# An eighth pair of buffers for the weighted expert products of a decoder block, and two small tiles fewer

## The chip, the cores and the metric

The kernel runs on one core of one Trainium2 chip. What is measured is the time of one execution on the device, in microseconds (us).

## What is computed

One block of a hybrid decoder on 1024 tokens of width 1024: two attention mixers, an attention to 256 memory tokens, and a channel mixer (PEER) with 16384 experts. Only the channel mixer matters here. Each token chooses 128 experts (8 heads of 16) and gets their weighted sum:

```python
a = jnp.einsum('cd,ced->ce', hc, u[ic])                  # first products: token times chosen rows of u
a = jax.nn.gelu(a, approximate=False) * gc               # weighted
return jnp.einsum('ce,ced->cd', a, v[ic])                # second products: weighted sum of chosen rows of v
```

All is in float32, with every product of large matrices made of three matmuls of a high and a low part (`mm3`, lines 135 to 137).

## The kernel before, in words

The channel mixer goes two ways at once. For tokens 0 to 511 (four blocks of 128) the chosen rows of u and v are **gathered**: GpSimd (POOL) issues an indirect DMA of 128 rows (512 KB), and VectorE (DVE) multiplies them with the tokens (line 1038, the u half) or adds them, weighted, to a sum (line 1057, the v half). There are 4 x 128 gathers of each kind, through 7 buffers `rows`. `gathered_u` leaves 128 first products per token in a tile `aa`, `gathered_v` makes weights `wexp` of it with a Gelu on ScalarE (ACT, line 1045) and a product with the gates (line 1046). The gathers are spread over the program beside other work.

For tokens 512 to 1023 the products are **dense** (function `dense`): all 16384 experts, in 128 steps of 128 experts, with the weight 0 for experts that a token did not choose. The weights lie in DRAM (`Wd`). A step has two halves.

- First products (`first`): the u rows of the step are loaded (`uraw`, 512 KB), split into a high part on ACT and a low part on DVE (`uT0`, `uT1`), and TensorE (PE) runs 24 matmuls into a PSUM tile `acc`. ACT applies Gelu (line 1253), DVE multiplies with the weights `wl` from `Wd` (line 1254; one load, 512 KB, serves two steps; there are two buffers `wl`), and the product is split again: high part `c0` on ACT (line 112), low part `c1` on DVE (line 113).
- Second products (`second`): the v rows are loaded (`vraw`) and split into `v0` (ACT) and `v1` (DVE), four buffers each, and PE runs 24 matmuls on `c0`, `c1`, `v0`, `v1`, into 8 PSUM outputs: four stay there (`kept`), four go through two buffers `out`, from which DVE adds them to a sum in SBUF (`accu`, line 1288).

Four steps make a **group**; there are 32. In a group's second half each of the 8 outputs takes 12 matmuls, so every one of its four `c` pairs is read until the last output. `group` of the next group is written ahead of `second` of this one, so that PE has the next first products or the next second products to go on with.

The first products of 48 steps, that is of 12 groups, were already made in an earlier stage and stored in DRAM (`ga`, after the Gelu). These **early groups** only load them (`c`, line 1250, one buffer of 256 KB) and multiply with `wl`. They are mixed among the others: the list `order` puts an early group at the places 2, 5, 7, 10, 13, 15, 18, 21, 23, 26, 29 and 31 (from 0).

So at 12 places PE finds no first products between two second halves. Call the groups around such a place P, X and E: E is early, X is the group ahead of it in the order, P the one ahead of X. PE goes from the second half of P straight to that of X; this is called a **crossing** below. X's steps are 0 to 3, and so are E's.

What stands on which engine in which order is set by a scheduler from the program's dependencies and its own costs; each engine then runs its queue in that order, and SyncE (SP) issues the loads in its own. A buffer that is not yet free makes the instruction that writes it wait, and what stands behind it on that queue. With `bufs=7`, four pairs `c0`, `c1` hold P's products and three X's; the pair of X's step 3 has to wait for the end of P's second half.

```python
w = w2[:, :, e % 2]                                                          # 1247: half of a tile wl
nc.vector.tensor_tensor(w, c.rearrange(...), w, op=OP.mult)                  # 1254
ch = [sp.tile([P, DT], F32R, name=f"c{j}", bufs=7) for j in range(2)]        # 1255
self.split(w, *[x.rearrange(...) for x in ch])                               # 1256
```

## Time and profile before

| what | value |
|---|---|
| median of 3 runs | 3581.61 us (3581.43 to 3586.86) |
| the profiled execution: its own time | 3578.94 us |
| the profiled execution: span of its instructions | 3577.2 us |
| busy in the span | PE 3049.6 us, DVE 2853.5 us, ACT 1405.0 us, POOL 1391.8 us |
| mean granted clock of PE | 0.921 of full speed |
| the dense loop | 2219 to 3545 us |

Times are microseconds from the span's start. An engine's idle time is put down to what ended it (the releaser). Matmuls overlap, so a sum of their durations is more than the time that they take in a row.

### The profile page before, as it was taken

What the parts mean: (1) busy time and instruction counts of PE and PEld (TensorE: products, weight loads), DVE (VectorE), ACT (ScalarE), POOL (GpSimd) and SP (SyncE); (2) the same over time, 40 slices, a digit from 0 to 9 for tenths busy, and PEclk for the clock granted to TensorE, in tenths of its full rate; (3) what the DMA queues carried; (4) which work ended last, traced back from release to release, by engine and by line L of the source; (5) the groups of instructions that cost most, each with busy time, mean ns of one, the idle gap of its engine ahead of it and who ended that gap; (6) DMA issues with size and microseconds to landing.
All of it is one profiled execution on the core that took longest, in us unless ns stands there. A gap on an engine that the chain in (4) does not pass through costs nothing. (4 is left out here: it accounts for less than half of the span.)

```text
span 3577.2 us, 42240 instructions
## 1 busy us (share of the span) xinstructions
PE 3049.6 (85%) x13234; PEld 2306.6 (64%) x13234; DVE 2853.5 (80%) x6623; ACT 1405.0 (39%) x2537; POOL 1391.8 (39%) x1122
## 2 busy tenths in 40 slices
PE   8999888798697997776998975888989898888995
PEld 7778756453355856465766764766777777676874
DVE  6656544698799889978998997887888888788987
ACT  5756344256575622132555564222222232222212
POOL 0010000002255265651125654465645546555554
PEclk9999989899897998888999988999999999899998
DMA  4584534436898398986569999999999999899987
GB/s 135 159 199 121 184 110 157 130 102 214 242 303 283 111 347 315 329 311 232 199 225 349 375 396 383 323 345 320 353 321 322 312 332 342 299 326 348 365 305 262
DMA packets 394209, 964.64 MB, mean 270 GB/s; under 512 B 36712, under 2 KB 146048, under 8 KB 392576
## 3 DMA queue, kind: packets, MB, share of 16 engines
q0 software_dynamic: 155264, 560.01, 44.7%
q1 hardware_dynamic: 238720, 401.94, 32.8%
q8 instruction: 104, 1.70, 0.2%
q14 instruction: 121, 0.99, 0.1%
HBM read 871.64 MB, written 90.18 MB: 269 GB/s over the span
## 5 line engine op out<-in xcount | busy, mean ns | idle before, releaser
L1035 POOL DMA_INDIRECT rows<-in_peer_u_dram,ii x512 | 681.2, 1331 | 925.6 <-DVE rows L1038 316.4
L1051 POOL DMA_INDIRECT rows<-in_peer_v_dram,ii x512 | 647.4, 1265 | 505.2 <-DVE h3s L1057 346.3
L1057 DVE SCALAR_TENSOR_TENSOR h3s<-rows,wexp,h3s 128x1024 f32<-128x1024 f32 x508 | 651.0, 1282 | 27.5 <-DMA rows<-in_peer_v_dram,ii 17.8
L1038 DVE SCALAR_TENSOR_TENSOR rows<-rows,h3s 128x1024 f32<-128x1024 f32 x512 | 610.3, 1217 | 61.4 <-DMA rows<-in_peer_u_dram,ii 59.8
L135 PE MATMUL acc<-fT,uT 128*128 128x512 f32 x1024 | 421.1, 411 | 65.5 <-DVE wl L1254 45.3
L137 PE MATMUL acc<-fT,uT 128*128 128x512 f32 x1024 | 412.2, 403 | 4.1 <-DVE uT L113 4.0
L136 PE MATMUL acc<-fT,uT 128*128 128x512 f32 x1024 | 413.7, 404 | 0.0
L112 ACT ACTIVATE c<-wl 128x512 fp32r<-128x512 f32 x128 | 79.4, 629 | 813.8 <-PE out L136 463.0
L135 PEld LDWEIGHTS acc<-fT,uT 128*128 128x128 f32 x1024 | 198.5, 194 | 112.6 <-issue 29.5
L149 POOL TENSOR_TENSOR rstd<-msq,mhalf 128x1 f32<-128x1 f32 (+1 forms) x42 | 34.1, 812 | 593.1 <-DVE msq L147 582.5
L136 PE MATMUL kept<-v,c 128*128 128x512 f32 x512 | 209.5, 410 | 61.3 <-DVE v L113 61.3
L135 PE MATMUL out<-v,c 128*128 128x512 f32 x512 | 210.7, 412 | 56.1 <-DVE accu L1288 56.1
L112 ACT ACTIVATE uT<-uraw 128x1024 fp32r<-128x1024 f32 x128 | 135.6, 1059 | 254.5 <-PE acc L136 194.5
L137 PEld LDWEIGHTS acc<-fT,uT 128*128 128x128 f32 x1024 | 197.4, 193 | 58.0 <-issue 11.2
L136 PEld LDWEIGHTS acc<-fT,uT 128*128 128x128 f32 x1024 | 198.4, 194 | 40.2 <-issue 0.8
L113 DVE TENSOR_TENSOR w<-wraw,w 128x512 fp32r<-128x512 f32 (+1 forms) x176 | 116.7, 679 | 116.8 <-ACT w L112 110.0
L137 PE MATMUL kept<-v,c 128*128 128x512 f32 x512 | 206.3, 403 | 0.0
L136 PE MATMUL out<-v,c 128*128 128x512 f32 x512 | 205.7, 402 | 0.0
L137 PE MATMUL out<-v,c 128*128 128x512 f32 x512 | 205.3, 401 | 0.0
L135 PE MATMUL kept<-v,c 128*128 128x512 f32 x512 | 203.5, 406 | 0.0
L568 ACT ACTIVATE junk<-W,xb 128x384 bf16<-128x384 f32 (+5 forms) x186 | 163.7, 880 | 77.0 <-DVE xb L566 65.5
L133 PE MATMUL acc<-wraw,hT 128*128 128x512 f32 (+1 forms) x384 | 170.4, 598 | 11.3 <-ACT tok L355 7.6
(361 smaller groups left out, 6717.8 us busy)
## 6 DMA issues: line engine op xcount, KB each, us to landing
uraw<-in_peer_ut_dram SPq DMA_DIRECT2D x128, 512.0 KB
vraw<-in_peer_v_dram SPq DMA_DIRECT2D x128, 512.0 KB
Wd<-wbuf SPq DMA_DIRECT2D x64, 512.0 KB
wl<-Wd SPq DMA_DIRECT2D x64, 512.0 KB
wraw<-in_w_in_dram SPq DMA_DIRECT2D x40, 512.0 KB
fraw<-in_w_in_dram SPq DMA_DIRECT2D x32, 512.0 KB
wraw<-in_w_out_dram SPq DMA_DIRECT2D x24, 512.0 KB
ga<-gelu SPq DMA_DIRECT2D x48, 256.0 KB
```

What stands on the lines that cost most here:

```text
L112: self.nc.scalar.activation(hi, src, AF.Copy)
L113: self.last_dve = self.nc.vector.tensor_tensor(lo, src, hi.bitcast(F32), op=OP.subtract).ins
L133: self.last_pe = nc.tensor.matmul(out, l[0], r[0], start=start, stop=stop).ins
L135: nc.tensor.matmul(out, l[0], r[0], start=start, stop=False)
L136: nc.tensor.matmul(out, l[0], r[1], start=False, stop=False)
L137: self.last_pe = nc.tensor.matmul(out, l[1], r[0], start=False, stop=stop).ins
L149: nc.gpsimd.tensor_tensor(r, v, self.mhalf[:, :n], op=OP.pow)
L568: nc.scalar.activation(junk[:, :(b + 1) * P], self.W[b], AF.Sign, bias=xb[:, j:j + 1].bitcast(F32), accum_out=s[:, j:j + 1])
L1035: nc.gpsimd.indirect_dma_start(out=u, out_offset=None, in_=a["peer_u"][0], in_offset=bass.IndirectOffsetOnAxis(ap=ii[:, j:j + 1], axis=0))
L1038: nc.vector.scalar_tensor_tensor(u, u, 1.0, h3, op0=OP.mult, op1=OP.mult, accum_out=aa[:, j:j + 1])
L1051: nc.gpsimd.indirect_dma_start(out=v, out_offset=None, in_=a["peer_v"][0], in_offset=bass.IndirectOffsetOnAxis(ap=r["ii"][:, j:j + 1], axi ...
L1057: nc.vector.scalar_tensor_tensor(o, v, w[:, j:j + 1], o, op0=OP.mult, op1=OP.add)
```

## The change

The pairs `c0`, `c1` get an eighth buffer (4 KB more per partition). To make room, `aa` has two buffers in place of three, and `gathered_v` makes its weights in place, in `aa`, so that `wexp` goes.

```diff
-        aa = r["aa"] = ep.tile([P, P], F32, name="aa", bufs=3)
+        aa = r["aa"] = ep.tile([P, P], F32, name="aa", bufs=2)
...
-        w = ep.tile([P, P], F32, name="wexp", bufs=1)
-        nc.scalar.activation(w, r["aa"], AF.Gelu)
+        w = r["aa"]
+        nc.scalar.activation(w, w, AF.Gelu)
         nc.vector.tensor_tensor(w, w, r["gg"], op=OP.mult)
...
-                    ch = [sp.tile([P, DT], F32R, name=f"c{j}", bufs=7) for j in range(2)]
+                    ch = [sp.tile([P, DT], F32R, name=f"c{j}", bufs=8) for j in range(2)]
```

No instruction is added or taken away, but the scheduler writes the queues in another order, at the crossings. Three places of the crossing at 2589 to 2640 us of the trace follow (its E is the fourth early group; P's `wl` is not in them, X's second tile is `wl_21477` before and `wl_21475` now, E's two tiles are `wl_21730` and `wl_21746` before and `wl_21727` and `wl_21743` now).

DVE at the crossing, before. `c1_21565` is X's step 3, `c1_21736`, `c1_21743` and `c1_21752` are E's steps 0 to 2, the `v1` are X's:

```order
L113 TENSOR_TENSOR c1_21565<-wl_21477,c0_21564 128x512
L1288 TENSOR_TENSOR accu_18901<-accu_18901,out_21713 128x512
L113 TENSOR_TENSOR c1_21736<-wl_21730,c0_21735 128x512
L113 TENSOR_TENSOR c1_21743<-wl_21730,c0_21742 128x512
L113 TENSOR_TENSOR v1_21763<-vraw_21764,v0_21762 128x1024
L113 TENSOR_TENSOR v1_21769<-vraw_21770,v0_21768 128x1024
L1254 TENSOR_TENSOR wl_21746<-c_21748,wl_21746 128x8x64
L113 TENSOR_TENSOR v1_21775<-vraw_21776,v0_21774 128x1024
L113 TENSOR_TENSOR c1_21752<-wl_21746,c0_21751 128x512
L113 TENSOR_TENSOR v1_21781<-vraw_21782,v0_21780 128x1024
```

X's step 3 is split at the crossing, and E's product of step 2, with the tile `wl_21746` that this split sets free, stands in the midst of X's four `v1`.

DVE in P's second half, ahead of the crossing, now. `c1_21563` is X's step 3, the products (line 1254) are E's steps 1 and 2:

```order
L1254 TENSOR_TENSOR wl_21727<-c_21736,wl_21727 128x8x64
L113 TENSOR_TENSOR uT1_21968<-uraw_21965,uT0_21967 128x1024
L113 TENSOR_TENSOR c1_21563<-wl_21475,c0_21562 128x512
L1038 SCALAR_TENSOR_TENSOR rows_21557,aa_19418<-rows_21557,h3s_19416 128x1024
L1288 TENSOR_TENSOR accu_18899<-accu_18899,out_21605 128x512
L1038 SCALAR_TENSOR_TENSOR rows_21554,aa_19418<-rows_21554,h3s_19416 128x1024
L1038 SCALAR_TENSOR_TENSOR rows_21551,aa_19418<-rows_21551,h3s_19416 128x1024
L1038 SCALAR_TENSOR_TENSOR rows_21602,aa_19418<-rows_21602,h3s_19416 128x1024
L1254 TENSOR_TENSOR wl_21743<-c_21745,wl_21743 128x8x64
```

The split of X's step 3 stands some 20 us earlier, and E's product of step 2 follows it after three gathered rows' products and one `accu`, then a fourth, still in P's second half. At the crossing itself there now stand E's four `c1` and then X's four `v1`, one behind the other.

SP, the loads around the same place, before:

```order
L1246 DMA wl_21730<-Wd_13635 128x8x128
L1205 DMA uraw_22059<-in_peer_ut_dram 128x1024
L1250 DMA c_21739<-ga13_14854 128x512
L1205 DMA uraw_22265<-in_peer_ut_dram 128x1024
L1250 DMA c_21748<-ga14_14957 128x512
L1246 DMA wl_21746<-Wd_13635 128x8x128
L1246 DMA wl_21923<-Wd_13635 128x8x128
L1270 DMA vraw_22107<-in_peer_v_dram 128x1024
```

and now:

```order
L1246 DMA wl_21727<-Wd_13634 128x8x128
L1205 DMA uraw_22056<-in_peer_ut_dram 128x1024
L1250 DMA c_21736<-ga13_14853 128x512
L1250 DMA c_21745<-ga14_14956 128x512
L1205 DMA uraw_22262<-in_peer_ut_dram 128x1024
L1246 DMA wl_21743<-Wd_13634 128x8x128
L1250 DMA c_21752<-ga15_15071 128x512
L1250 DMA c_22605<-ga16_15163 128x512
L1246 DMA wl_21920<-Wd_13634 128x8x128
L1246 DMA wl_22011<-Wd_13634 128x8x128
L1270 DMA vraw_22104<-in_peer_v_dram 128x1024
```

E's second tile `wl` is still the next load of weights, but it is now let go by the split of X's step 3 in P's second half, directly behind a load of u (`uraw_22262`) whose buffer the row before that split on DVE sets free. The early products of E's step 3 are loaded ahead of the crossing too.

## Rows read from the trace of the kernel before

**Rows 1.** The page's first line.

```profile
span 3577.2 us, 42240 instructions
```

**Rows 2.** Three stretches: start and end, length, then for each engine the busy time (and instructions), the granted clock of PE, the busy share of the DMA engines, GB/s. The dense loop, and two stretches behind a stall of PE.

```profile
2219.00:3545.00 1326.00, 1191.87 (x4944) 959.79 (x4944) 1113.47 (x1384) 327.19 (x428) 718.27 (x535) 0.94 0.92 328
...
2636.00:2640.00 4.00, 3.69 (x9) 2.95 (x10) 3.79 (x5) 0.00 (x0) 0.54 (x1) 0.50 0.94 336
...
2645.00:2660.00 15.00, 15.00 (x68) 12.40 (x67) 14.19 (x15) 4.43 (x5) 10.90 (x9) 1.00 0.82 278
```

**Rows 3.** DVE in the dense loop (2219 to 3545 us), groups of instructions by line: count, busy us, mean ns of one, then the idle time ahead of them and what ended it.

```profile
L1057 DVE SCALAR_TENSOR_TENSOR h3s<-rows,wexp,h3s 128x1024 f32<-128x1024 f32 x274 | 351.1, 1282 | 5.4 <-DMA rows<-in_peer_v_dram,ii 0.2
L1038 DVE SCALAR_TENSOR_TENSOR rows<-rows,h3s 128x1024 f32<-128x1024 f32 x256 | 303.3, 1219 | 29.6 <-DMA rows<-in_peer_u_dram,ii 28.2 <-issue 0.7
L113 DVE TENSOR_TENSOR v<-vraw,v 128x1024 fp32r<-128x1024 f32 x128 | 151.7, 1217 | 0.3 <-ACT v L112 0.2
L113 DVE TENSOR_TENSOR c<-wl,c 128x512 fp32r<-128x512 f32 x128 | 86.7, 686 | 0.5 <-ACT c L112 0.5
L1288 DVE TENSOR_TENSOR accu<-accu,out 128x512 f32<-128x512 f32 x123 | 83.7, 680 | 9.0 <-PE out L137 8.8
L1254 DVE TENSOR_TENSOR wl<-c,wl 128x512 f32<-128x512 f32 x48 | 33.1, 689 | 158.0 <-DMA wl<-Wd 131.8 <-DMA c<-ga 14.4 <-issue 11.6
```

**Rows 4.** What PE waited for in the dense loop: us in total, times, longest.

```profile
PE kept L136 <- DVE v L113: 61.3, 19, 6.3
PE out L135 <- DVE accu L1288: 56.1, 22, 5.6
PE acc L135 <- DVE wl L1254: 45.3, 7, 29.1
```

**Rows 5.** DVE in order of time: start, length, line, operation; in brackets how long the engine had been idle and what ended it.

```profile
2258.16 0.69 DVE L1254 TENSOR_TENSOR wl<-c,wl 128x512 f32<-128x512 f32 x1 [5.51 <-DMA wl<-Wd]
...
2288.72 0.69 DVE L1254 TENSOR_TENSOR wl<-c,wl 128x512 f32<-128x512 f32 x1 [3.85 <-issue]
...
2470.35 0.69 DVE L1254 TENSOR_TENSOR wl<-c,wl 128x512 f32<-128x512 f32 x1 [9.64 <-DMA wl<-Wd]
...
2602.08 0.69 DVE L1254 TENSOR_TENSOR wl<-c,wl 128x512 f32<-128x512 f32 x1 [7.16 <-DMA wl<-Wd]
...
2624.28 0.68 DVE L113 TENSOR_TENSOR c<-wl,c 128x512 fp32r<-128x512 f32 x1
...
2626.73 2.39 DVE L113 TENSOR_TENSOR v<-vraw,v 128x1024 fp32r<-128x1024 f32 x2
2634.43 0.69 DVE L1254 TENSOR_TENSOR wl<-c,wl 128x512 f32<-128x512 f32 x1 [5.32 <-DMA wl<-Wd]
2635.04 1.22 DVE L113 TENSOR_TENSOR v<-vraw,v 128x1024 fp32r<-128x1024 f32 x1
...
2926.67 0.69 DVE L1254 TENSOR_TENSOR wl<-c,wl 128x512 f32<-128x512 f32 x1 [5.14 <-DMA wl<-Wd]
...
3470.13 0.69 DVE L1254 TENSOR_TENSOR wl<-c,wl 128x512 f32<-128x512 f32 x1 [2.54 <-DMA wl<-Wd]
...
3503.36 0.69 DVE L1254 TENSOR_TENSOR wl<-c,wl 128x512 f32<-128x512 f32 x1 [4.94 <-DMA wl<-Wd]
```

**Rows 6.** SP's queue in order of time: start, length and count of the issues. A row with x2 runs from the first issue to the end of the second.

```profile
2281.42 0.37 SPq L1246 DMA_DIRECT2D wl<-Wd  x1
...
2447.92 6.83 SPq L1205 DMA_DIRECT2D uraw<-in_peer_ut_dram  x2
2454.97 0.38 SPq L1246 DMA_DIRECT2D wl<-Wd  x1
...
2582.66 6.10 SPq L1205 DMA_DIRECT2D uraw<-in_peer_ut_dram  x2
2589.00 0.38 SPq L1246 DMA_DIRECT2D wl<-Wd  x1
...
2624.99 2.21 SPq L1246 DMA_DIRECT2D wl<-Wd  x2
...
2914.20 0.33 SPq L1065 DMA_DIRECT2D rows<-x  x1
2915.98 0.33 SPq L1205 DMA_DIRECT2D uraw<-in_peer_ut_dram  x1
2916.53 0.38 SPq L1246 DMA_DIRECT2D wl<-Wd  x1
```

**Rows 7.** PE in order of time, matmuls alone; in brackets the idle time and what ended it.

```profile
2290.60 0.50 PE L136 MATMUL kept<-v,c 128*128 128x512 f32 x1 [1.36 <-DVE v L113]
...
2620.44 0.50 PE L135 MATMUL out<-v,c 128*128 128x512 f32 x1 [2.49 <-DVE accu L1288]
...
2625.62 0.80 PE L135 MATMUL out<-v,c 128*128 128x512 f32 x1 [3.98 <-DVE accu L1288]
...
2636.31 0.80 PE L136 MATMUL kept<-v,c 128*128 128x512 f32 x1 [3.90 <-DVE v L113]
...
3505.24 0.50 PE L136 MATMUL kept<-v,c 128*128 128x512 f32 x1 [3.08 <-DVE v L113]
```

**Rows 8.** POOL in order of time: the gather behind the load of weights at 2916.53 us.

```profile
2928.83 1.86 POOL L1035 DMA_INDIRECT rows<-in_peer_u_dram,ii  x1 [13.85 <-DVE h3s L1057]
```

**Rows 9.** What ACT waited for, over the dense loop: us in total, times, longest.

```profile
ACT c L112 <- PE out L136: 463.0, 29, 22.9
```

## The prediction

> **What bounds the kernel now.** I read the page first, then the stretches, then what each engine waited for in the dense loop, and last the timelines of one crossing. The change can only act in the dense loop, 1326 us of the span of 3577.2 us [rows 1, 2]: ahead of it the queues stand as they stood. In the loop PE is the engine that nearly fills the time. Its waits there are named: 61.3 us for a split of v, 56.1 us for `accu`, and, of the third row, 16.2 us once its longest wait of 29.1 us, which ends as the loop begins, is taken off [rows 4]. The reader is to see that all three are ended by DVE. DVE in turn waits for loads: of its idle time, 158.0 us lie ahead of the 48 products of the early groups, nearly all of it for the weights `wl` (131.8 us, and 11.6 us put down to "issue" at the same products), while the gathered rows cost 28.2 us and PE 8.8 us [rows 3]. ACT waits 463.0 us in 29 pieces for the end of a second half, with a `c0` that has no buffer [rows 9]; ACT has nothing to do in that time, so this alone is worth nothing.
>
> The 143.4 us at the early products fall into two kinds, 12 of each. The **first wait** is at E's step 0: the first is 5.51 us at 2258.16 us, the last 2.54 us at 3470.13 us [rows 5], and the 12 make 85.2 us. The **second wait** is at E's step 2, in the midst of the crossing: the first is 3.85 us at 2288.72 us, the last 4.94 us at 3503.36 us [rows 5], and the 12 make 58.3 us.
>
> What each costs PE is read from one crossing. The load for the first wait is issued at 2589.00 us and ends it at 2602.08 us, after 7.16 us of idle DVE [rows 5, 6]. DVE is late from there on, and PE pays at 2620.44 and 2625.62 us with 2.49 and 3.98 us [rows 7]. Then the split of X's step 3 at 2624.28 us frees the other tile, SP issues the load at 2624.99 us, DVE does two of X's four `v1`, sits idle for 5.32 us until 2634.43 us, and the third `v1` follows at 2635.04 us [rows 5, 6]. PE, which had matmuls on the first two `v1` to do, waits only 3.90 us, until 2636.31 us [rows 7]. The 12 gaps of this second sort run from 1.36 us at 2290.60 us to 3.08 us at 3505.24 us [rows 7] and make 31.6 us. The rest of PE's waits for `accu` and v is 61.3 + 56.1 - 31.6 = 85.8 us: as much as the first waits' 85.2 us. So **a wait of DVE ahead of the crossing reaches PE whole; one in the midst of the `v1` reaches it by half** (31.6 of 58.3 us).
>
> **The change part by part.** `aa` and `wexp`: the u half of block b+2 writes the tile whose weights the v half of block b has long used, since the halves alternate; the Gelu and its product run as before. I cost this at nothing. The cover is the v half of block b+1, 128 gathers long; without it the next u half would wait for that.
>
> The eighth pair takes away the wait of X's step 3 for P's end. Four terms follow from the order of the queues, with durations from [rows 3] (0.6 us between starts for the short DVE instructions, since they overlap a little, 1.2 us for a split of v, 1.2 to 1.3 us for a gathered row).
>
> 1. The second wait leaves the crossing: X's four `v1` now stand in a row. **-31.6 us.**
>
> 2. It comes back ahead of the crossing, in P's second half. The tile is freed by the split of X's step 3, as before; between that split and E's product of step 2 DVE has 4.7 us of work on the mean of the 12 places now, 4.2 us before. How long the load takes there no row shows, so I bound it. The 12 second loads before took 58.3/12 + 4.2 = 9.0 us on the mean, the shortest 7.3 us (2281.42 to 2288.72 us); none had a load of u just ahead on SP's queue. The 12 first loads, most of which have one 0.6 us ahead, took 85.2/12 + 5.8 (DVE's work between) = 12.9 us, the longest 15.4 us (2454.97 to 2470.35 us) [rows 5, 6]. The moved load has a load of u about as close ahead of it. But DVE has just stood still for the first wait, so few gathers are in flight. The nearest row is the load at 2916.53 us: `uraw` 0.55 us ahead, another 512 KB at 2914.20 us, no gather issued behind it until POOL goes on at 2928.83 us after 13.85 us; it took 10.1 us [rows 5, 6, 8]. I take 9.6 us, between this and 9.0 us, because the moved load has one transfer fewer ahead on its queue but some gathers behind. That is 4.9 us of wait, whole to PE: **+58.8 us** (bounds: 7.3 us of landing gives 31 us, 12.9 us gives 98 us, and 0 if it lands in time).
>
>    The Trainium skill, in "DMA: Bandwidth & Descriptors", section "Anatomy of one DMA", fits one transfer as 2.0 us and its bytes at 436 GB/s; worked out for 512 KB that is an estimate of 3.2 us, and by it the term would be nothing and the whole sum a gain. The trace disagrees at every load named here: none landed in under 7.3 us beside the gathers [rows 5, 6].
>
> 3. DVE reaches X's first `v1` later, since E's products and splits of steps 2 and 3 now stand ahead of it and one gathered row fewer: 26.5 us of work behind E's step 0 against 24.9 us. PE has on the mean 2.9 us of matmuls ahead of the first that needs it, against 2.1 us, because first products are drawn forward at 7 crossings rather than 5. 1.6 - 0.8 = 0.8 us, 12 times: **+9.6 us** (bounds 0 and 20 us).
>
> 4. At the first wait DVE has 5.4 us of work between split and product, against 5.8 us: **+4.3 us**. The early products of step 3, which cost DVE part of the 14.4 us before, stay at nothing: their load has about 3 us of DVE work to hide it, and if it takes longer, the rest is a further wait ahead of the crossing, some 1 us each.
>
> The clock gives no term. Behind a gap PE runs at half its clock (0.50 from 2636 to 2640 us, the lower of its two levels) and is back at 1.00 from 2645 us [rows 2]; there are about as many gaps as before. One slow start more or less at each crossing would be about 2 us each, 24 us either way at most.
>
> Sum: -31.6 + 58.8 + 9.6 + 4.3 = **+41.1 us**. On the profiled execution's 3578.94 us that is 3620.0 us; the median of the three runs lies 2.67 us above that execution, so I forecast 3622 us.
>
> **The rivals.**
>
> *The load lands in time* (faster). After the first wait the gathers' queue has run dry, the moved load meets empty DMA engines, and the second wait is simply gone. Then terms 1, 3 and 4 are left: -17.7 us, 3564 us. The point from which it decides is a landing in 4.7 + 17.7/12 = 6.2 us. For it: POOL really stops when DVE does [rows 8], and the load no longer shares the crossing with other loads of weights and v. Against it: no load of weights in these rows came under 7.3 us, and the loop's DMA engines are 0.92 busy [rows 2]. The fit of "DMA: Bandwidth & Descriptors" named above would bring this case about.
>
> *DVE sets the pace, and its waits only move* (no change). DVE's busy time and its waits together fill the loop, and it waits for PE for only 8.8 us [rows 2, 3]. If that holds behind the crossing too, 58.3 us of second waits become 58.8 us, and only term 4 is left: 3586 us. Against it: PE runs at 1.00 without a gap from 2645 to 2660 us [rows 2], so there DVE is not what it waits for.
>
> *The moved load is as slow as the first ones* (slower still). With 12.9 us the wait is 8.2 us, 12 times 98.4 us, and the sum +80.7 us: 3662 us. It is what the `uraw` ahead of it speaks for.
>
> *Nothing moves.* The queues do differ, so this needs every crossing to come out even by accident: 3582 us.
>
> **How the numbers follow.** Forecast 0.47, load in time 0.23, waits only move 0.12, slow load 0.15, nothing moves 0.03. A difference of 0.2% (7 us) is about what a measurement of this kernel can tell from no change. Slower: 0.47 + 0.15 = 0.62; faster 0.23; same 0.15. The range takes in the gain of the first rival and the bound of the slow load, 3563 to 3660 us; outside lie the parts of these two cases beyond their own values, about 0.16 together. The forecast's own range, from a landing of 7.3 us to one of 11.5 us, is 3595 to 3645 us.
>
> **What would show it.** In the changed kernel's profile: ACT's wait with `c0` for the end of a second half is still there, but at E's step 0; DVE's idle time at the early products is still some 140 us, with both waits now ahead of the crossing; PE's waits for v have lost the sort in the midst of a crossing, and its waits for `accu` have grown. If DVE's idle time at these products falls to about 90 us, the first rival is right. The prediction is wrong if the second loads land in under 6.2 us, or if PE's waits for `accu` and v together fall below 117 us.

## The result, and the profile after

The change makes the kernel faster by 0.7%: 3556.6 us (median, 3546.93 to 3563.5) against 3581.61 us, ratio 0.9926 [0.9902, 0.9951]. In a later comparison the same kernel took 3546.55 us against 3578.55 us, ratio 0.9906 [0.9885, 0.9928]. The forecast was 3622 us, slower, with a range from 3563 us: it had the sign wrong.

The profiled execution took 3556.62 us, and its instructions span 3554.6 us, 22.6 us less than before [rows 1]. (It has 50 instructions fewer, 42190 in all; the 50 are waits for semaphores.) The stretch ahead of the dense loop took 10 us more in this execution. So the loop is what fell. Its stretch after, and the four microseconds behind a gap of PE (columns as in [rows 2]):

```profile
2229.00:3528.00 1299.00, 1181.39 (x4944) 957.80 (x4944) 1118.39 (x1389) 329.78 (x428) 717.69 (x539) 0.95 0.93 337
2628.00:2632.00 4.00, 4.00 (x12) 3.21 (x13) 2.83 (x4) 2.73 (x4) 2.79 (x2) 0.65 0.51 155
```

The loop lost 27 us at the same work: 1326 us before, 1299 us now. What DVE waited at the early products (line 1254, the row that answers to the last of [rows 3]):

```profile
L1254 DVE TENSOR_TENSOR wl<-c,wl 128x512 f32<-128x512 f32 x48 | 33.2, 691 | 123.1 <-DMA wl<-Wd 103.2 <-DMA c<-ga 19.6
```

158.0 us became 123.1 us. PE's waits (they answer to [rows 4]), and ACT's for the end of a second half, with a `c0` (to [rows 9]) and with a `v0`:

```profile
PE out L135 <- DVE accu L1288: 84.8, 31, 7.6
PE acc L135 <- DVE wl L1254: 34.9, 5, 28.7
PE kept L136 <- DVE v L113: 24.9, 5, 10.3
```

```profile
ACT v L112 <- PE out L137: 371.5, 17, 28.0
...
ACT c L112 <- PE out L136: 157.1, 20, 18.1
```

The waits for v have lost 36.4 us and those for `accu` have gained 28.7 us. The second row, without the wait of 28.7 us ahead of the loop, fell from 16.2 to 6.2 us. ACT stands 157 us with a `c0` instead of 463 us, but now 371.5 us with a `v0` whose buffer a second half still reads: its wait has moved on to the next buffer that is short.

The crossing of [rows 5 to 7] now, DVE, then SP, then PE, in order of time:

```profile
2603.57 0.69 DVE L113 TENSOR_TENSOR c<-wl,c 128x512 fp32r<-128x512 f32 x1
2610.88 0.69 DVE L1254 TENSOR_TENSOR wl<-c,wl 128x512 f32<-128x512 f32 x1 [6.62 <-DMA wl<-Wd]
...
2616.15 0.68 DVE L113 TENSOR_TENSOR c<-wl,c 128x512 fp32r<-128x512 f32 x1
...
2626.28 0.69 DVE L1254 TENSOR_TENSOR wl<-c,wl 128x512 f32<-128x512 f32 x1 [4.28 <-DMA wl<-Wd]
...
2638.47 1.29 DVE L113 TENSOR_TENSOR c<-wl,c 128x512 fp32r<-128x512 f32 x2
2639.67 0.68 DVE L1288 TENSOR_TENSOR accu<-accu,out 128x512 f32<-128x512 f32 x1
2640.27 1.29 DVE L113 TENSOR_TENSOR c<-wl,c 128x512 fp32r<-128x512 f32 x2
2641.47 4.62 DVE L113 TENSOR_TENSOR v<-vraw,v 128x1024 fp32r<-128x1024 f32 x4
```

```profile
2598.51 0.38 SPq L1246 DMA_DIRECT2D wl<-Wd  x1
...
2616.30 0.33 SPq L1205 DMA_DIRECT2D uraw<-in_peer_ut_dram  x1
2616.85 0.37 SPq L1246 DMA_DIRECT2D wl<-Wd  x1
```

```profile
2627.83 0.80 PE L135 MATMUL out<-v,c 128*128 128x512 f32 x1 [3.45 <-DVE accu L1288]
2628.42 0.63 PE L136 MATMUL out<-v,c 128*128 128x512 f32 x1
2628.85 0.63 PE L137 MATMUL out<-v,c 128*128 128x512 f32 x1
...
2634.77 0.50 PE L135 MATMUL out<-v,c 128*128 128x512 f32 x1 [2.31 <-DVE accu L1288]
...
2640.41 0.79 PE L135 MATMUL out<-v,c 128*128 128x512 f32 x1 [4.21 <-DVE accu L1288]
```

The order is the one forecast: X's step 3 is split at 2616.15 us in P's second half, the moved load goes out at 2616.85 us, 0.55 us behind a load of u, and E's product of step 2 waits 4.28 us for it. At the crossing E's four `c1` and X's four `v1` stand in a row, and PE has no wait for v there. All its gaps, 10.0 us here, are waits for `accu`, ahead of the crossing and at it. The starts of the two matmuls at 2628.42 and 2628.85 us are 0.43 us apart; at full clock it is 0.226 us.

So the loop can be taken apart. Its time (from the start of PE's first matmul behind its long wait to the start of the last) is 4943 spacings of 0.226 us, which make 1117 us, plus PE's idle time, plus what is left of each spacing beyond 0.226 us when the idle time in it is taken off. This is a way to add up the time, not a test of anything. The last part is called half clock below, because most of it is the half clock behind gaps; 4 to 6 us of it in each profile are spacings of under 0.3 us. The waits of DVE are its idle time at E's four steps, 12 products each. The old order with seven pairs and the change have two profiles each.

| kernel | us, ratio [interval] | loop | PE idle | half clock | DVE's waits at E's steps 0, 1, 2, 3 |
|---|---|---|---|---|---|
| before | 3581.61 | 1325.7 | 133.9 | 74.8 | 85.2, 1.3, 58.3, 13.1 |
| seven pairs again (`c7_inplace`) | 3581.2, 1.0012 [0.9997, 1.0028] | 1312.6 | 124.2 | 71.3 | 80.8, 0.8, 55.7, 12.7 |
| the change | 3556.6, 0.9926 [0.9902, 0.9951] | 1297.7 | 116.6 | 64.0 | 66.7, 2.3, 49.2, 4.6 |
| the change again (`c8_again`) | 3546.55, 0.9906 [0.9885, 0.9928] | 1295.2 | 120.5 | 57.7 | 67.5, 2.9, 42.7, 9.5 |
| `c7_wl3` | 3536.62, 0.9886 [0.9866, 0.9906] | 1283.9 | 109.7 | 57.2 | 36.2, 20.0, 32.3, 5.8 |
| `c8_v3raw` | 3615.87, 1.0097 [1.0076, 1.0117] | 1367.8 | 162.2 | 88.6 | 54.6, 5.3, 39.0, 13.8 |
| `c8_wl3` | 3619.98, 1.0114 [1.0089, 1.0140] | 1370.5 | 163.0 | 90.4 | 58.9, 0.9, 43.8, 6.3 |
| `c8_behind` | 3478.34, 0.9719 [0.9699, 0.9739] | 1230.9 | 71.3 | 42.6 | 0, 47.3, 5.5, 19.0 |
| `c7_behind` | 3504.88, 0.9800 [0.9777, 0.9823] | 1254.9 | 84.8 | 53.1 | 0, 57.9, 1.6, 28.7 |
| `c8_nowl` | 3488.36, 0.9738 [0.9714, 0.9762] | 1234.4 | 74.5 | 42.8 | 0, 31.9, 0.6, 24.4 |
| `c7_nowl` | 3513.2, 0.9820 [0.9799, 0.9841] | 1254.9 | 84.7 | 53.2 | 0, 42.5, 0, 52.2 |
| `c7_behind_g3` | 3477.21, 0.9725 [0.9705, 0.9746] | 1221.9 | 64.1 | 40.7 | 0, 0, 22.4, 36.3 |
| `c8_behind_g3` | 3506.39, 0.9810 [0.9791, 0.9829] | 1233.7 | 69.3 | 47.2 | 0, 0, 0, 22.8 |
| `c8_wlact` | 3552.75, 0.9925 [0.9901, 0.9948] | 1300.7 | 120.9 | 62.7 | 71.6, 2.1, 38.7, 10.6 |
| `c7_wlact` | 3631.81, 1.0157 [1.0137, 1.0177] | 1365.2 | 163.2 | 85.0 | 105.0, 0.6, 91.0, 1.5 |
| `c8_r5` | 3647.44, 1.0205 [1.0180, 1.0230] | 1331.4 | 141.1 | 73.2 | 54.5, 4.1, 33.1, 11.0 |
| `c8_spaced` | 3460.47, 0.9685 [0.9661, 0.9709] | 1206.8 | 51.3 | 38.4 | 0, 3.6, 33.0, 15.0 |

Each ratio is against the kernel before on the same chip (its medians there: 3575.0 to 3581.6 us). In the loop `c7_inplace` has DVE's order of the kernel before, and `c8_again` that of the change, instruction by instruction. Every other kernel that is compared with one of these got another order from the scheduler along with its edit, so its difference is that of both together.

### The profile page after: what moved, and what is told of

It is laid out like the page before. It is cut to its first block, busy times and chain, and to the rows that moved or that the text cites. A ratio compares the mean times of both kernels' runs of the same rounds, so it can differ in the third digit from the quotient of the medians.

```text
span 3554.6 us, 42190 instructions
## 1 busy us (share of the span) xinstructions
PE 3039.4 (86%) x13234; PEld 2305.0 (65%) x13234; DVE 2851.8 (80%) x6623; ACT 1406.4 (40%) x2537; POOL 1388.4 (39%) x1122
## 3 DMA queue, kind: packets, MB, share of 16 engines
q1 hardware_dynamic: 238720, 401.94, 33.1%
## 4 chain that ended last, share of the span: by engine, by line
PE 33%; DVE 25%; DMA 17%; issue 14%; POOL 6%; ACT 4%; SPq 1%; POOLq 0%; DVEq 0%; ACTq 0%
PE acc L135 5%; PE acc L136 5%; PE acc L137 5%; DMA wl<-Wd 5%; POOL rows L1035 4%; DVE h3s L1057 4%; DVE rows L1038 3%; DMA so<-pq 2%; DMA rows<-in_peer_v_dram,ii 2%; DMA rows<-in_peer_u_dram,ii 2%; PE po L727 2%; DMA c<-ga 2%; POOL rows L1051 2%; DMA fraw<-in_w_in_dram 1%; DVE uT L113 1%
## 5 line engine op out<-in xcount | busy, mean ns | idle before, releaser
L1035 POOL DMA_INDIRECT rows<-in_peer_u_dram,ii x512 | 671.4, 1311 | 914.8 <-DVE rows L1038 292.1
L1057 DVE SCALAR_TENSOR_TENSOR h3s<-rows,aa,h3s 128x1024 f32<-128x1024 f32 x508 | 651.4, 1282 | 32.2 <-DMA rows<-in_peer_v_dram,ii 23.1
L1038 DVE SCALAR_TENSOR_TENSOR rows<-rows,h3s 128x1024 f32<-128x1024 f32 x512 | 611.4, 1220 | 59.3 <-DMA rows<-in_peer_u_dram,ii 58.8
L135 PE MATMUL acc<-fT,uT 128*128 128x512 f32 x1024 | 420.2, 410 | 55.7 <-DVE wl L1254 34.9
L112 ACT ACTIVATE v<-vraw 128x1024 fp32r<-128x1024 f32 x128 | 126.2, 1046 | 406.2 <-PE out L137 371.5
L135 PE MATMUL out<-v,c 128*128 128x512 f32 x512 | 213.6, 417 | 84.9 <-DVE accu L1288 84.8
L137 PEld LDWEIGHTS acc<-fT,uT 128*128 128x128 f32 x1024 | 198.1, 193 | 57.6 <-issue 10.9
L136 PE MATMUL kept<-v,c 128*128 128x512 f32 x512 | 202.9, 397 | 24.9 <-DVE v L113 24.9
L137 PE MATMUL kept<-v,c 128*128 128x512 f32 x512 | 201.5, 394 | 0.0
L135 PE MATMUL kept<-v,c 128*128 128x512 f32 x512 | 198.3, 396 | 0.0
```

What stands on the lines that cost most here:

```text
L112: self.nc.scalar.activation(hi, src, AF.Copy)
L135: nc.tensor.matmul(out, l[0], r[0], start=start, stop=False)
L136: nc.tensor.matmul(out, l[0], r[1], start=False, stop=False)
L137: self.last_pe = nc.tensor.matmul(out, l[1], r[0], start=False, stop=stop).ins
L1035: nc.gpsimd.indirect_dma_start(out=u, out_offset=None, in_=a["peer_u"][0], in_offset=bass.IndirectOffsetOnAxis(ap=ii[:, j:j + 1], axis=0))
L1038: nc.vector.scalar_tensor_tensor(u, u, 1.0, h3, op0=OP.mult, op1=OP.mult, accum_out=aa[:, j:j + 1])
```

## The experiments

### Is it the pair?

`c7_inplace` is the change without its third edit:

```diff
-                    ch = [sp.tile([P, DT], F32R, name=f"c{j}", bufs=8) for j in range(2)]
+                    ch = [sp.tile([P, DT], F32R, name=f"c{j}", bufs=7) for j in range(2)]
```

> Seven pairs c as before, with the other half of the change alone: aa two buffers, the weights made in place. Theory 'crossing' (the gain comes from the eighth pair, which takes the product of E's step 2 out of X's four v1): no change from the kernel before, within 0.2%, 3575 to 3588 us; PE's waits for v in the dense loop about 61 us, for accu about 56 us. Rival 'tiles' (the smaller tiles or the weights made in place bring the gain): about 3557 us.

Ratio 1.0012: no difference. The pair does it, and the tiles cost nothing. Its profile is also a second one of the old order: PE waits 57.0 us for v and 54.3 us for `accu`.

`c8_again` is the change unaltered.

> The changed kernel once more, for a second profile of it. If what fell in the first profile comes from the order of the queues, DVE's waits at E's step 0 (85.2 and 80.8 us in two profiles with seven pairs, 66.7 us with eight) come out at 60 to 73 us again, and PE's waits for accu and v together at 105 to 115 us; the time is 3545 to 3565 us. If the 18 us less at step 0 were an accident of one execution, they come out at 78 to 90 us.

67.5 us at step 0 again: the 16 us less there belong to the order. PE's waits for `accu` and v make 115.8 us, just over the stretch given.

### Does DVE's waiting for weights cost what PE loses?

`c7_wl3` spends the 4 KB on a third tile `wl` (`bufs=7` for c, and on line 1245 `bufs=3`).

> Seven pairs c, and the 4 KB of the eighth pair spent on a third tile wl instead, so that each load of weights is let go one tile earlier, some 20 to 40 us; the wait of X's step 3 for P's end stays. Theory 'weights' (what DVE waits for wl at the early products, 143 us before and 116 us now, is what PE pays for): DVE's idle time at these products falls from 158 to under 40 us (what is left is the early products c), PE's waits for accu from 56 to under 20 us, the sort in the crossing goes too, and the time is 3581 - 36 - 32 - some 20 of half clock = about 3490 us (3470 to 3520). Rival 'DMA' (the engines are 0.92 busy in the loop, so what no longer waits for weights waits for gathered rows or for v and u): DVE's waits for gathered rows grow from 33 us to over 100 us, and the time stays over 3560 us.

3536.6 us: a little better than the change by the ratio, with intervals that overlap, and not by what was expected. DVE's waits fell to 94 us, not under 40 us; PE's waits for v fell to 18.6 us, those for `accu` stayed at 53.0 us. The rows of DVE, then of SP, at its fourth early group show why the waits did not go:

```profile
2563.90 0.69 DVE L113 TENSOR_TENSOR c<-wl,c 128x512 fp32r<-128x512 f32 x1
...
2572.53 0.69 DVE L1254 TENSOR_TENSOR wl<-c,wl 128x512 f32<-128x512 f32 x1 [2.81 <-issue]
```

```profile
2564.61 0.38 SPq L1246 DMA_DIRECT2D wl<-Wd  x1
```

The load goes out as soon as a split lets its tile go, and the scheduler has moved the early product up behind it: between the two DVE has 5 to 6 us of work, as in the kernel before. Load and product both come some 25 to 30 us earlier than in [rows 5, 6], so the buffer more gave the load no more time to land. The rival does not explain it either: DVE waits 32.4 us for gathered rows of u, 28.2 us before [rows 3].

`c8_v3raw` has eight pairs and three buffers `vraw` in place of four (`V_BUFS = (4, 4, 3)`); `c8_wl3` has a third `wl` as well.

> Eight pairs as in the change, and the raw rows of v with three buffers instead of four: it prices the buffer that the next kernel gives up for a third wl. Theory 'crossing' and theory 'weights': the fourth load of X's v starts later, so PE's waits for v grow by 0 to 3 us at each of 12 crossings, 3557 to 3595 us. Rival 'DMA': fewer transfers side by side, wl lands earlier, 3545 to 3557 us.

> Eight pairs, a third tile wl, and the raw rows of v with three buffers to make room. Theory 'weights': the 116 us of waits at E's steps 0 and 2 go, PE's waits for accu fall from 85 to under 25 us and half clock by some 20 us, so 80 us less than the kernel with eight pairs and three buffers of raw v: 3480 to 3510 us. Rival 'DMA': within 15 us of that kernel, with over 60 us more of waits for gathered rows.

The buffer given up costs 60 us, more than any bound I gave. X's fourth load of v can go out only when one of the three tiles is free. In `c8_v3raw` the waits of ACT for the load, and of DVE for ACT's split of v:

```profile
ACT v L112 <- DMA vraw<-in_peer_v_dram: 290.2, 33, 17.6
...
DVE v L113 <- ACT v L112: 96.0, 34, 5.3
```

In the kernel after, ACT waits 1.8 us for that load. With a third `wl` on top nothing is won (3620 us): E's waits stay at 110 us, since the product moves up again (at step 0 DVE has 5.6 us of work between the split and the product). The waits for gathered rows did not grow (15.9 us), so it is not the DMA engines.

`c8_behind` keeps every transfer and holds the early products back: E's group is written behind X's second half, and its four products are queued on DVE behind X's last `v1`.

```diff
-                nx = group(order[k + 1]) if k + 1 < n else None
+                late = k + 1 < n and order[k + 1] < m
+                nx = group(order[k + 1]) if k + 1 < n and not late else None
                 second(gi, cs)
-                cs = nx
+                cs = group(order[k + 1]) if late else nx
...
+                    with self.tc.issue_after(at) if e in ga else ExitStack():
-                    nc.vector.tensor_tensor(w, c.rearrange("p (j n) -> p j n", j=2 * ND), w, op=OP.mult)
+                        nc.vector.tensor_tensor(w, c.rearrange("p (j n) -> p j n", j=2 * ND), w, op=OP.mult)
```

(`at` is the last split on DVE when the group is begun.) `c7_behind` is the same with seven pairs.

> Eight pairs; E's group is written behind X's second half, and E's four early products are queued on DVE behind X's last v1, so that the loads of wl have the rest of P's second half to land in. All transfers stay. Theory 'weights' (DVE is late because the scheduler moves an early product up to where its buffer comes free, so that its load is always late, and PE pays for most of that): DVE's waits at the early products fall from 123 to under 20 us, PE's waits for accu from 85 to under 30 us, half clock by some 20 us: 3460 to 3500 us. Rival 'DMA': gathered rows, v and u come later by what is gained, DVE's waits for rows grow from 32 to over 80 us, and the time stays over 3535 us.

> The same order with seven pairs: X's step 3 is split at the crossing after P's end, and only then the load for E's step 2 goes out, with some 9 us of DVE's work ahead of its product. Theory 'weights': DVE's waits at the early products under 30 us, and the eighth pair is worth only the wait for the pair of X's step 3, 1 to 3 us at each crossing: 12 to 36 us more than the kernel with eight pairs in this order. Rival: the eighth pair is worth in this order what it is worth in the other, 23 to 27 us, because what it takes away (the late v1) is there in both.

3478 us, a ratio of 0.9719. The waits for `wl` are gone from the loop but for its first load; PE's waits for `accu` with them. DVE's waits at the early products fell to 72 us, not under 20 us. PE, and DVE, from 2200 us to the end of `c8_behind`:

```profile
PE acc L135 <- DVE wl L1255: 70.8, 12, 28.9
PE kept L136 <- DVE v L113: 18.5, 10, 3.4
PE out L135 <- DVE accu L1289: 5.9, 5, 4.0
```

```profile
DVE wl L1255 <- DMA c<-ga: 71.7, 27, 6.3
DVE rows L1038 <- DMA rows<-in_peer_u_dram,ii: 20.7, 19, 4.8
DVE wl L1255 <- DMA wl<-Wd: 9.9, 1, 9.9
```

What is left is the wait for `c`, whose one buffer is loaded only when the product ahead has read it. The gathered rows do not come later (20.7 us). So it was the place of the early products that made DVE late, and the DMA engines did not bound the loop, although their share rose:

```profile
2213.00:3445.00 1232.00, 1159.90 (x4944) 944.60 (x4944) 1112.96 (x1387) 330.57 (x428) 708.45 (x537) 0.97 0.97 354
```

With seven pairs in this order it takes 26.5 us more. That lies inside what both theories had given. DVE's waits at the early products are 88 us there, not under 30 us. The reason that the rival gave, the late v1, does not hold: PE waits less for v than with eight pairs, not more. Two of PE's rows in `c7_behind`:

```profile
PE out L135 <- DVE accu L1289: 16.8, 6, 4.1
...
PE kept L136 <- DVE v L113: 5.0, 2, 4.2
```

`c8_nowl` and `c7_nowl` leave out the early groups' loads of `wl` and do not hold the products back; the order of DVE's queue comes out otherwise in them all the same:

```diff
+                        if e not in ga:
-                        nc.sync.dma_start(w2, self.Wd[:, :, e:e + 2].rearrange("j p e n -> p j e n"))
+                            nc.sync.dma_start(w2, self.Wd[:, :, e:e + 2].rearrange("j p e n -> p j e n"))
...
-                    nc.vector.tensor_tensor(w, c.rearrange("p (j n) -> p j n", j=2 * ND), w, op=OP.mult)
+                    cw = c.rearrange("p (j n) -> p j n", j=2 * ND)
+                    nc.vector.tensor_tensor(w, cw, cw if e in ga else w, op=OP.mult)
```

> Eight pairs in the order of the change, but the weights of the early groups are left out: their 24 loads of wl are not made, and the early products are multiplied with themselves. It leaves out 12.6 MB of some 435 MB of the loop. Theory 'weights': the 103 us of DVE's waits for wl go, the early products c (20 us) may come late instead: PE's waits for accu from 85 to under 35 us, 3460 to 3500 us. Rival 'DMA': only the time of the transfers left out, 3% of the loop or at most 40 us, 3515 us or more. Rival 'half' (a wait of DVE ahead of the crossing reaches PE only in part): between the two.

> Seven pairs in the order of the kernel before, with the weights of the early groups left out: their 24 loads of wl are not made, and the early products are multiplied with themselves. Theory 'crossing' (the eighth pair's own worth is the late v1 of the crossing, whatever the weights do): 20 to 35 us more than the 3488 us with eight pairs and no such loads, with PE's waits for v over 35 us against 11 us. Rival: without the waits for weights the eighth pair is worth nothing, under 8 us.

PE in `c8_nowl`, then in `c7_nowl`:

```profile
PE out L135 <- DVE accu L1290: 54.2, 23, 4.3
PE acc L135 <- DVE wl L1256: 37.1, 7, 29.6
PE kept L136 <- DVE v L113: 11.5, 3, 4.6
```

```profile
PE acc L135 <- DVE wl L1256: 50.6, 10, 29.1
PE kept L136 <- DVE v L113: 35.0, 13, 5.1
PE out L135 <- DVE accu L1290: 25.8, 12, 4.3
```

`c8_nowl` lies where theory 'weights' had it, though PE's waits for `accu` fell to 54 us only, not under 35 us. With eight pairs, 65.8 us less of DVE's waits (122.7 on the mean of two profiles to 56.9 us) took 44 us from PE's idle time and 18 us from the half clock: 62 us of the loop, nearly one for one, but PE's idle time alone fell by two thirds of what DVE's waits did.

Between seven and eight pairs lie 24.8 us. So the pair is worth 25.0 and 32.0 us as it was made, 26.5 us with the products held back and 24.8 us without the loads: **25 to 32 us in these three settings**. In each of them PE's idle time is 10 to 14 us less and the half clock 10 to 12 us. Which wait carries it differs. Without the loads, PE's waits for v are 23.5 us less and those for first products (without the long wait) 14 us less, but those for `accu` 28.4 us more. With the products held back, v costs 13.5 us more, `accu` 10.9 us and first products 7 us less. So the late v1 of the crossing is not what the pair is worth by itself, and why the balance comes out alike is not shown.

### What does a load wait behind?

The load for E's step 0 landed in 12.7 and 12.5 us in the two profiles with seven pairs, and in 10.8 and 10.9 us with eight (12 loads each, from SP's issue to DVE's product). The ninth early group is a place with a large difference. SP and DVE there, before, and the stretch of the load:

```profile
3134.74 0.38 SPq L1246 DMA_DIRECT2D wl<-Wd  x1
...
3149.88 0.69 DVE L1254 TENSOR_TENSOR wl<-c,wl 128x512 f32<-128x512 f32 x1 [9.11 <-DMA wl<-Wd]
```

```profile
3134.71:3149.86 15.15, 15.15 (x68) 12.57 (x67) 5.86 (x10) 3.73 (x5) 4.17 (x4) 1.00 1.02 384
```

and after:

```profile
3119.77 0.38 SPq L1246 DMA_DIRECT2D wl<-Wd  x1
...
3131.63 0.69 DVE L1254 TENSOR_TENSOR wl<-c,wl 128x512 f32<-128x512 f32 x1 [7.86 <-DMA wl<-Wd]
```

```profile
3119.75:3131.63 11.88, 11.88 (x54) 9.85 (x53) 4.02 (x6) 3.73 (x5) 3.42 (x3) 1.00 1.02 383
```

The DMA engines are full and as fast in both: 384 and 383 GB/s. What differs is how much they move until the load is there: 15.15 us by 384 GB/s is 5.8 MB, 11.88 us by 383 GB/s is 4.5 MB. Over the 12 loads it is 4.65 and 4.60 MB with seven pairs, 3.89 and 3.97 MB with eight. A load of 0.5 MB lands with six to eight other transfers' worth of traffic ahead of or beside it. Its own packets are neither served at once nor all last: they begin 4.4 us behind the issue with seven pairs and 3.3 us with eight, and the last begins at 11.9 and 10.2 us (means of two profiles). Of the 0.7 MB less, 0.4 MB are gathered rows and 0.3 MB other loads of SP, by the DMA queues, about in the proportion in which they stood. At a given rate the bytes follow from the time, so this alone does not say what the load waits behind; the next kernels ask that.

The load that landed soonest in this profile fits: E's step 2 at the seventh early group, after the change, where POOL has just stood still. It is issued at 2930.01 us. DVE and the stretch:

```profile
2934.19 0.69 DVE L1254 TENSOR_TENSOR wl<-c,wl 128x512 f32<-128x512 f32 x1 [1.27 <-DMA wl<-Wd]
```

```profile
2930.00:2934.24 4.24, 4.24 (x21) 3.50 (x20) 2.97 (x4) 1.15 (x2) 0.00 (x0) 1.00 0.59 174
```

The engines are busy at 0.59 only, 0.7 MB is moved, and the load takes 4.2 us. The 3.2 us worked out from the Trainium skill ("DMA: Bandwidth & Descriptors", section "Anatomy of one DMA — SWDGE (gpsimd) path"), an estimate for a transfer by itself, comes near here and at one more of the 24 loads (4.6 us). The page gives its fit for transfers that GpSimd issues, and SP issues this one, so no run here tests the fit itself. At the other 22 places the load took 7.0 us or more.

`c8_r5` has five gather buffers (`R_BUFS` 5 for 7).

> The changed kernel with five gather buffers instead of seven, to see what the weights' load waits behind. Theory 'queue' (a load lands when what was issued ahead of it has been moved): at E's step 0 some 5.7 MB are issued in the 15 us ahead of it, 1 MB of it goes: landing from 10.8 to about 9 us, DVE's waits there from 67 to 45 us or less; at step 2, where few gathers are under way, no change from 46 us within 8 us. Rival 'no queue': landing at step 0 stays within 0.8 us of 10.8. DVE's waits for gathered rows grow in either case, and the time with them.

Landing 10.1 us, 0.7 us less: by the measure given, the gathers are not what the load waits behind, or only a little. DVE's waits fell to 54.5 us at step 0 and, against both theories, to 33.1 us at step 2; the gathered rows cost 97 us, and the whole takes 3647.4 us, ratio 1.0205 [1.0180, 1.0230], with some 50 us of the loss ahead of the loop.

`c8_wlact` and `c7_wlact` issue the early groups' loads of `wl` from ACT (`nc.scalar.dma_start` on line 1246 for `e in ga`, eight and seven pairs).

> The changed kernel, with the 24 loads of wl of the early groups issued by ACT instead of SP. Theory 'own queue' (the load lands late because it stands behind the four loads of v and two of u that SP issued in the 15 us ahead): landing at E's step 0 falls from 10.8 to 5 to 8 us and DVE's waits there from 67 to under 35 us; at step 2, with one load of u ahead, from 8.3 to 6 or 7 us, waits from 46 to under 30 us; 3490 to 3520 us. Rival 'engines' (it shares the DMA engines with everything, 0.93 busy): landing within 1 us of 10.8 and 8.3 us, no change of the time beyond 10 us but for what ACT, held up by the wait for the tile, does later.

> Seven pairs (with the smaller tiles), the same 24 loads issued by ACT. 'Own queue': landing at step 0 from 12.5 to 5 to 8 us, as with eight pairs, so that the eighth pair's gain at step 0 (18 us of DVE's waits) is gone, since nothing of SP's is ahead of the load in either; the eighth pair is then worth the crossing's v1 alone. 'Engines': 12 to 13 us, and the difference to eight pairs at step 0 stays near 18 us.

The first of the 12 loads for step 0 of `c8_wlact`, on ACT's queue, and the product behind it on DVE:

```profile
2257.39 0.39 ACTq L1246 DMA_DIRECT2D wl<-Wd  x1
```

```profile
2266.67 0.69 DVE L1254 TENSOR_TENSOR wl<-c,wl 128x512 f32<-128x512 f32 x1 [4.40 <-DMA wl<-Wd]
```

It took 9.3 us, the 12 on the mean 10.5 us, and the time does not change: at step 0 the load does not wait behind SP's own queue, but behind or beside what the DMA engines have on hand. Those for step 2 took 7.2 us, 1.1 us less than the 8.3 us named, in neither band. With seven pairs it lands later (13.2 us at step 0, 11.9 us at step 2), and a difference stays, 2.7 us of landing at step 0, which speaks for the rival; but in DVE's waits there it is 33 us, not 18 us.

The time grew by 50 us against seven pairs with SP as issuer, and here the pair is worth 79 us. The rows of ACT and of PE in `c7_wlact` show where it went:

```profile
PE kept L136 <- DVE v L113: 90.0, 18, 8.3
...
ACT v L112 <- DVE c L113: 64.4, 12, 9.3
```

The issue on ACT's queue has to wait until DVE's split of X's step 3 lets the tile go. ACT stands there 64.4 us at the 12 crossings with X's splits of v behind it, and PE's waits for v grow from 57.0 to 90.0 us, those for `accu` from 54.3 to 69.9 us. Why fewer bytes stand ahead of the load with eight pairs stays open.

### What is left, and a version that beats both

`c7_behind_g3` is `c7_behind` with three buffers `c`; `c8_behind_g3` is `c8_behind` with three, and six gather buffers to make room.

> Early products behind the crossing's v1 as in the last kernels, seven pairs, and the 4 KB of the eighth pair spent on two more buffers for the early groups' first products c (three instead of one), whose loads now end 88 us of DVE's waits. Theory 'loads' (what is left at the early products is that each c is loaded only when the one ahead of it has been used): these waits fall from 88 to under 15 us, PE's waits that DVE's products end (49 us) to under 20 us, and with half clock the time falls by 50 to 80 us, to 3425 to 3455 us. Rival 'pair': the split of X's step 3 stands in the crossing, and with E's products close behind it DVE is only late in another place: 3485 us or more.

> The same with eight pairs and three buffers c; room comes from one gather buffer fewer (six rows). Theory 'loads': DVE's waits for c from 72 to under 15 us, PE's from 42 to under 20 us, and half clock in proportion: 3425 to 3450 us, 10 to 30 us less than with seven pairs. Rival 'gathers': with six buffers the gathered rows come late, DVE's waits for them grow from 26 to over 60 us, and nothing is won over the 3478 us of the kernel with one c.

Seven pairs with three `c` equal eight with one: 3477.2 us. The waits fell from 88 to 59 us in all, not under 15: at step 2 its `wl` is late (the tile comes free at the crossing), and step 3 waits 36.3 us for `c`. PE's waits for first products fell from 49 to 35 us, not under 20 us, so the time is between the two theories. With eight pairs the waits for `c` fell to 22.8 us, but the loop did not get shorter (1233.7 us). DVE in `c8_behind_g3`:

```profile
DVE rows L1038 <- DMA rows<-in_peer_u_dram,ii: 47.7, 41, 4.0
DVE h3s L1057 <- DMA rows<-in_peer_v_dram,ii: 27.4, 41, 1.8
```

75 us in place of 26 us: the rival 'gathers' holds, and the loop begins later, at 2232 us (2214 us in `c8_behind`).

`c8_spaced` needs no buffer. It queues E's four products behind four given instructions:

```diff
-                cs, at = [], self.last_dve
+                cs, v = [], self.last_dve
+                at = [(self.past or [v] * 4)[2], v] + self.adds[:2]
...
-                    with self.tc.issue_after(at) if e in ga else ExitStack():
+                    with self.tc.issue_after(at[e % G]) if e in ga else ExitStack():
```

(`adds` and `past` are the additions to `accu` of X's and P's second halves.)

> Early products behind given work, as in the kernel at 3478 us, but spread: E's step 0 behind P's third addition to accu, step 1 behind X's last v1, steps 2 and 3 behind X's first and second addition. Theory 'loads': with one buffer c a product has to stand a load (3.5 to 6 us) behind the one ahead of it; DVE's waits for c, 72 us (47 of them at step 1), fall to under 25 us, PE's waits from 71 us to under 50 us, and with half clock the time to 3420 to 3455 us. Rival: the product of step 0 is so early again that its wl is late, or its split stands ahead of P's end and holds up the v1 of the crossing; then the waits only move, and the time is 3470 us or more.

3460.5 us, ratio 0.9685 [0.9661, 0.9709]: 3.2% less than the kernel before, and the lowest median here, with an interval that just overlaps those of `c8_behind` and `c7_behind_g3`. The wait at step 1 went from 47.3 to 3.6 us, but step 2 took 33.0 us, so DVE's waits fell only to 52 us, not under 25 us, and the time stayed 5 us above what was expected. PE's idle time in the loop is 51.3 us.

## Why the forecast was wrong

Means of two profiles of either order, in the loop, against the terms:

| what | forecast | measured |
|---|---|---|
| term 1: PE's waits for v at the crossing | -31.6 | 59.1 to 24.3 us, -34.8 |
| terms 2 to 4, all as waits for `accu` | +72.7 | 55.2 to 88.5 us, +33.3 |
| PE's first products waiting for DVE (second row of [rows 4]) | 0 | 14.2 to 5.1 us, -9.1 |
| half clock | 0 | 73.0 to 60.8 us, -12.2 |
| sum | +41.1 | -22.8 (the loop: -22.7) |

**`aa` and `wexp` at nothing:** right, by `c7_inplace`.

Terms 2 to 4 came out 39 us too large, and two rows that the forecast put at nothing gave 21 us. Why PE waited 9.1 us less for DVE at its first products is not shown.

**Term 1:** right, in place and size.

**Term 2:** the mechanism was right, the size too large. The wait came back where it was said to, and DVE waits 49.2 and 42.7 us there, 46 us on the mean instead of 58.8 us. 12.7 and 11.4 us of this, at two of the twelve places, are waits for `c`, not for the load of weights. From the issue to the product it took 8.6 and 8.1 us, not 9.6 us. At the six places with a load of u about 0.55 us ahead, as in the order rows that I looked at, it took 9.8 us on the mean of the first profile (the two that waited for `c` are among them); at the other six, where SP has something else ahead, 7.4 us. I took one place for all twelve.

**Term 4, the step that failed most:** E's first wait was to grow by 4.3 us and shrank by 16 us, from 83.0 to 67.1 us. I counted DVE's work between split and product and left the landing at 12.9 us, as if it belonged to the load. With eight pairs it landed in 10.8 us, against 12.6 us on the mean of two profiles with seven, with 0.7 MB less moved until then: the landing goes with the traffic around the load, and the change moves that too. This is read from the two orders; `c8_r5` and `c8_wlact`, which took away gathers and SP's queue, changed the landing by 0.7 and 0.3 us only.

**"A wait of DVE ahead of the crossing reaches PE whole":** held about by the totals, as it was read. After the change all of DVE's waits lie ahead of it, 122.7 us on the mean, and PE's for `accu` and v make 112.7 us. Where DVE's waits for the weights were taken away (`c8_nowl`, with its own order of the queue), 44 of 65.8 us came off PE's idle time, not the whole. Term 3 cannot be seen: the waits at steps 0 and 2 give 46.0 - 15.9 = 30.1 us of the 33.3 us.

**"The clock gives no term":** wrong, by 12 us, inside the 24 us that were named as the most. The gaps became 42 and 43 in place of 48 and 47, and each carried 1.3 to 1.6 us of half clock. By `c8_behind` and `c8_nowl`, 47 and 44 us of PE's idle time took 18 us of half clock each with them.

**The rivals.** "The load lands in time" gave 3564 us, the nearest, but not by its reason: from the issue to the product it took 8.6 us, not under 6.2 us, and the second wait is still there. "Waits only move" had half of the truth: PE's waits for v and `accu` nearly cancel (-34.8 and +33.3 us), but DVE's waits fell by 31 us, and the time with PE's first products and the half clock. The "slow load" did not occur.

**The tests named.** ACT's wait with `c0` for the end of a second half is still there, 157 us in place of 463 us. DVE's idle time at the early products is 123 us: between the 140 us of the forecast and the 90 us of the first rival. PE's waits for `accu` and v are 109.7 and 115.8 us, under the 117 us below which the forecast was to be wrong.

## What to carry to other kernels

When a buffer is added under a scheduler that issues what is ready first, look at what moves up into it: the consumer of a late load moves with the buffer and still waits (94 us in `c7_wl3`), and holding it back by an ordering edge gained 68 us more (`c8_behind`) where the buffer had given 25 to 32 us. Do not carry a load's landing time from one order to another: beside full engines it went with the bytes moved around it. (No run here forecast a landing from such bytes; they were read afterwards.) And price an idle microsecond of PE together with the half clock behind it, here about 1.4 us together.

## What the runs showed of the hardware

Beside full DMA engines a 512 KB load took 10.8 to 12.7 us, in which 3.9 to 4.7 MB were moved at about 365 GB/s, and issued by another engine at step 0 it took about the same (10.5 against 10.8 us, with eight pairs). A share of 0.92 was no bound: in the loop of `c8_spaced` it is 0.99 at 362 GB/s, with PE busy for 0.96 of the time against 0.90 before:

```profile
2224.00:3431.00 1207.00, 1155.57 (x4944) 938.41 (x4944) 1112.31 (x1387) 330.35 (x428) 706.90 (x538) 0.98 0.99 362
```

PE's idle time was not paid alone in any of these profiles: beside 51 to 163 us of it, spacings of more than 0.226 us between the starts of matmuls added 38 to 90 us.
